# Probabilities times values of the first attention head group: one float32 product per head half instead of two split parts

## The chip, the cores and the metric

The kernel runs on one core of one Trainium2 chip. The metric is device time in microseconds (us) of one execution. Before the change three runs took 2131.02, 2131.66 and 2137.23 us, a median of 2131.66 us.

## The reference

An encoder of two layers over 1024 tokens of width 1024, all in float32. Each layer has three mixers side by side, an output projection, and a gated feed-forward part. The part that the change touches is the windowed attention: eight query heads in two groups of four, each group with one key/value head of width 64, and a window of three blocks of 128 tokens.

```python
kb, vb = bands(k), bands(v)                      # three neighbouring blocks of 128
qb = q.reshape(b, nb, BLOCK, N_KV_HEADS, grp, HEAD_DIM)
scores = jnp.einsum('bnqhgd,bnjhd->bnhgqj', qb, kb) * (HEAD_DIM ** -0.5)
probs = jax.nn.softmax(jnp.concatenate([scores, sink_b], axis=-1), axis=-1)[..., :-1]
out = jnp.einsum('bnhgqj,bnjhd->bnqhgd', probs, vb)
...
x = x + rmsnorm(concat([rmsnorm(y_f), rmsnorm(y_a), rmsnorm(y_m)]) @ w_out)
gate, up = jnp.split(rmsnorm(x) @ w_ffn_in, 2, axis=-1)
x = x + rmsnorm((silu(gate) * up) @ w_ffn_out)
```

## The kernel before

The tokens are worked in eight tiles of 128. Large products keep float32 accuracy with operands split in two: `split` (L149) writes the rounded high part with ScalarE (L151) and the rest with a subtraction on VectorE or GpSimd (L152), both in the type fp32r, and the product is the sum of the products of the parts. Working memory is two hand-placed arenas, `arena_r` (fp32r) and `arena_f` (float32), in which `at(k, ...)` and rings of places k name the buffers; a pool `big` holds more. PSUM has four pools of two banks: `sc`, `pT`, `av`, `pd`.

A layer runs in stages. After the Fourier mixer, the key/value and query products and the memory attention comes the stage of **head group 0** of the window attention, woven by `weave` with the projection of the Fourier and memory parts (tile `mo`, L162, results to the DRAM buffer `pmd`). Then follows the stage of **head group 1**, written out tile by tile together with the projection of the attention part (`mo` again, L1008), the residual and two norms (L324, L325, L284, L289), the transposes of the normed tile (`hTp`, L1033), and sums for the feed-forward part. That part begins with products named `qy`, `qz`, `qx`, `qw` (L1104), whose weights are loaded into places of arena_f that tiles 5 and 6 leave free, and summed on VectorE (L1094).

Each attention unit n of a group does the scores (`sc`, L728), masks and maxima on VectorE (L729, L735), exponentials on ScalarE (L741), and the division on GpSimd (L752). One unit later `att_values` (L756) takes for each of two or three key blocks j the transposes of four heads into one bank `pT` (L765), brings them to SBUF, and multiplies with the values into `av`. There are 22 key blocks for a group in a layer, 88 in all. The two groups do that last step differently:

- **Group 0**: `split` of the 128x512 block (high part on ScalarE, L151; low part on VectorE, L152), then two fp32r products of 128x512 (L780), whose stationary operand holds the high and the low part of the values side by side. So rows 0 to 63 of `av` hold the product with one part, rows 64 to 127 with the other. `fold` (L795) copies one half with ScalarE (L801) and adds the other with VectorE (L802), twice per unit, and thereby puts even heads into partitions 0 to 63 and odd heads into 64 to 127.
- **Group 1**: one copy by ScalarE (L770) that sorts even and odd heads, then two float32 products of 128x256 (L773) with the 64 columns of the float32 values, one for the even heads into the partitions 0 to 63 of `av` and one for the odd heads into 64 to 127. One copy by ScalarE (L782) ends the unit. The float32 values are made in advance by `values_32` (L786) on GpSimd (L791).

A float32 product stands in the profile as two matmul records, so a pair of products (even and odd heads) is four records of L773.

The order of instructions on each engine is chosen by the compiler's scheduler from the program order, the dependencies and its own estimate of durations. Every engine then works off its own queue in that order.

Of the kernel before, what the change touches and what calls it, by code (L numbers as in the profile page):

```python
# [68 lines left out]
def tile_encoder(ctx: ExitStack, tc: tile.TileContext, T, C, out):  # L69
# [51 lines left out]
    def run(k, n, step):  # L121
        return Ring(*[k + i * step for i in range(n)])
# [12 lines left out]
    mps, phs, yys = run(24, 2, 4), run(16, 3, 4), run(104, 2, 4)  # L135
# [332 lines left out]
    class Mix:  # L468
# [288 lines left out]
        def att_values(self, g, n, es_, dst):  # L757
# [4 lines left out]
            for j in range(nk):  # L762
# [3 lines left out]
                if g:  # L766

                    pf = self.pfs[self.pfi % 4]
                    self.pfi += 1
                    nc.scalar.copy(pf, pT.rearrange("p (k s) q -> p s k q", s=2))  # L770
                    for s in range(2):
                        rhs = pf[:, s].rearrange("p k q -> p (k q)")
                        mm(av[64 * s : 64 * s + 64, 0 : 2 * P], self.v32[:, k0 + j], rhs, start=j == 0, stop=j == nk - 1)  # L773
                    continue
                pp = phs(2, 512, dt=F32R)
                ph, pl = pp[:, 0], pp[:, 1]
                split(ph, pl, pT.rearrange("p h q -> p (h q)"))
                lhs = self.vst[(k0 + j) // 4][:, (k0 + j) % 4, g].rearrange("p a d -> p (a d)")
                for i, p_ in enumerate((ph, pl)):
                    mm(av, lhs, p_, start=j == 0 and i == 0, stop=j == nk - 1 and i == 1)  # L780
            if g:
                nc.scalar.copy(dst, av[:, 0 : 2 * P].rearrange("p (k q) -> p k q", k=2))  # L782
            else:
                self.fold(av, dst)

        def values_32(self):  # L786

            self.v32 = at(4, NT, HD)
            for half in range(2):
                v = self.vst[half][:, :, 1]  # L790
                nc.gpsimd.tensor_tensor(out=self.v32[:, 4 * half : 4 * half + 4], in0=f32(v[:, :, 0]), in1=f32(v[:, :, 1]), op=ALU.add)  # L791
            pf = big(4, 2, 2, P, dt=F32)
            self.pfs, self.pfi = [pf[:, i] for i in range(4)], 0

        def fold(self, av, dst):  # L795

            cut = lambda ap: ap.rearrange("p (h s q) -> p s h q", s=2, q=P)
            avh, avl = cut(av[0:64]), cut(av[64:128])
# [133 lines left out]
        def fm_load(self):  # L932
            sqs.ks = (16, 18)
            self.wfm = self.load_wout((0, 1, 6, 7))
# [520 lines left out]
```

## Time and profile before

| what | value |
|---|---|
| median of three runs | 2131.66 us |
| the profiled execution, time | 2135.5 us |
| its span, first to last instruction | 2133.7 us |
| mean granted TensorE clock | 0.969 |
| TensorE matmul busy | 2013.2 us, 94% of the span |
| VectorE busy | 1577.7 us, 74% |
| ScalarE busy | 1060.6 us, 50% |
| GpSimd busy | 863.4 us, 40% |

The profile names PE (TensorE matmul), PEld (its weight loads), DVE (VectorE), ACT (ScalarE), POOL (GpSimd), SP (SyncE) and L-numbers, which are lines of the kernel before. A timeline row is: start, length, engine, line, operation, output tile, inputs, shapes, number of instructions merged, and in brackets how long the engine was idle before and what ended that. In layer 0 the stage of group 0 lies at about 228 to 306 us of the span and that of group 1 at 306 to 410 us; in layer 1 at about 1285 to 1363 us and 1363 to 1475 us.

### The profile page before, as it was taken

To read this page: it belongs to the slowest core of one execution; us is meant where nothing else is said; L and a number is where in the kernel's file an instruction comes from. 1 tells how busy PE (TensorE), PEld (TensorE's weight loads), DVE (VectorE), ACT (ScalarE), POOL (GpSimd) and SP (SyncE) were. 2 spreads that over 40 slices of the span, in tenths; PEclk is the share of its full clock that TensorE was granted. 3 is DMA by queue.
4 is the path that set the end of the run, shared out by engine and by line. 5 is a ranking of instruction groups with operands and counts; after the bars stand their busy time and mean duration, and the time that the engine had idled before them with its cause. 6 is when DMAs were issued, how large, how long until landed. Compare 5 with 4: busy or idle time off the path is not lost.

```text
span 2133.7 us, 28334 instructions
## 1 busy us (share of the span) xinstructions
PE 2013.2 (94%) x9490; PEld 1655.0 (78%) x9490; DVE 1577.7 (74%) x2441; ACT 1060.6 (50%) x2257; POOL 863.4 (40%) x858
## 2 busy tenths in 40 slices
PE   7998999699999999999989989996999999999997
PEld 6887887478888887878868768775888888878785
DVE  7568756898877877657875686578987787876774
ACT  6467776553333334444544677776433333345441
POOL 4244446653423434213453444475442333431322
PEclk9998999899999999999989989998999999999998
DMA  6112123422332326968731122243232232378874
GB/s 221 45 50 65 65 94 105 152 65 94 118 101 95 112 94 194 318 221 287 246 138 41 60 64 85 75 137 110 84 129 94 94 111 92 123 249 284 276 261 138
DMA packets 173602, 287.50 MB, mean 135 GB/s; under 512 B 15480, under 2 KB 73360, under 8 KB 173456
## 3 DMA queue, kind: packets, MB, share of 16 engines
q1 hardware_dynamic: 165392, 266.82, 38.1%
q10 hardware_dynamic: 8064, 18.88, 2.3%
q8 instruction: 74, 1.21, 0.2%
q14 instruction: 72, 0.59, 0.1%
HBM read 219.06 MB, written 66.58 MB: 134 GB/s over the span
## 4 chain that ended last, share of the span: by engine, by line
PE 74%; DMA 8%; DVE 7%; ACT 4%; POOL 4%; issue 2%; SPq 0%; POOLq 0%; DVEq 0%; ACTq 0%
PE fo L1232 12%; PE qz L1104 11%; PE qx L1104 11%; PE qy L1104 11%; PE mo L162 7%; PE qw L1104 5%; PE kvp L162 4%; PE qp L162 3%; DVE arena_r L152 3%; DMA arena_f<-actd 2%; PE sc L728 2%; PE pT L765 2%; DMA arena_f<-in_w_ffn_out 1%; ACT arena_r L151 1%; PE zT L162 1%
## 5 line engine op out<-in xcount | busy, mean ns | idle before, releaser
L151 ACT CAST arena_r<-arena_f 128x512 fp32r<-128x512 f32 (+1 forms) x780 | 443.1, 591 | 674.0 <-PE qz L1104 115.5
L152 DVE TENSOR_TENSOR arena_r<-arena_f,arena_r 128x512 fp32r<-128x512 f32 (+1 forms) x676 | 536.6, 816 | 182.9 <-ACT arena_r L151 179.6
L1232 PE MATMUL fo<-arena_r 128*128 128x512 f32 x1848 | 432.2, 395 | 17.5 <-ACT arena_r L151 15.1
L1232 PEld LDWEIGHTS fo<-arena_r 128*128 128x128 f32 x1848 | 351.7, 191 | 94.6 <-ACT arena_r L151 17.7
L1104 PE MATMUL qy<-arena_r 128*128 128x512 f32 x1056 | 261.5, 397 | 27.6 <-ACT arena_r L151 16.5
L1104 PEld LDWEIGHTS qy<-arena_r 128*128 128x128 f32 x1056 | 201.5, 192 | 72.0 <-ACT arena_r L151 17.0
L1094 DVE TENSOR_TENSOR arena_f<-arena_f 128x512 f32<-128x512 f32 x220 | 206.0, 939 | 5.1
L1104 PE MATMUL qz<-arena_r 128*128 128x512 f32 x704 | 196.3, 389 | 1.8 <-DVE arena_r L152 1.8
L1124 POOL TENSOR_TENSOR arena_f<-arena_f 128x512 f32<-128x512 f32 x44 | 73.0, 1658 | 292.8 <-ACT arena_f L1109 292.8
L1216 POOL TENSOR_TENSOR arena_f<-arena_f 128x512 f32<-128x512 f32 x50 | 73.6, 1475 | 269.5 <-DVE arena_r L152 136.2
L1104 PEld LDWEIGHTS qz<-arena_r 128*128 128x128 f32 x704 | 132.0, 188 | 29.8 <-DVE arena_r L152 2.4
L1156 POOL TENSOR_TENSOR arena_f<-arena_f 128x512 f32<-128x512 f32 x44 | 73.6, 1674 | 165.6 <-DVE arena_f L1136 119.1
L152 POOL TENSOR_TENSOR arena_r<-arena_f,arena_r 128x256 fp32r<-128x256 f32 (+2 forms) x104 | 88.8, 859 | 118.4 <-ACT arena_r L151 93.3
L1104 PE MATMUL qx<-arena_r 128*128 128x512 f32 x528 | 127.7, 389 | 1.4 <-ACT arena_r L151 1.4
L1104 PE MATMUL qw<-arena_r 128*128 128x512 f32 x528 | 127.6, 389 | 0.0
L1104 PE MATMUL qx<-big,arena_r 128*128 128x512 f32 x528 | 126.8, 389 | 0.0
L1104 PEld LDWEIGHTS qx<-arena_r 128*128 128x128 f32 x528 | 99.1, 188 | 22.5 <-ACT arena_r L151 2.0
L1104 PE MATMUL qz<-big,arena_r 128*128 128x512 f32 x352 | 115.5, 389 | 0.0
L1104 PEld LDWEIGHTS qw<-arena_r 128*128 128x128 f32 x528 | 99.1, 188 | 20.8
L1104 PEld LDWEIGHTS qx<-big,arena_r 128*128 128x128 f32 x528 | 99.1, 188 | 20.6
L162 PE MATMUL mo<-arena_r 128*128 128x512 f32 x384 | 102.6, 406 | 5.5 <-POOL arena_r L152 4.0
L162 PE MATMUL mo<-big,arena_r 128*128 128x512 f32 x384 | 102.3, 404 | 0.0
(223 smaller groups left out, 3558.1 us busy)
## 6 DMA issues: line engine op xcount, KB each, us to landing
arena_f<-in_w_ffn_out SPq DMA_DIRECT2D x264, 256.0 KB, 4.3
arena_f<-in_w_ffn_in SPq DMA_DIRECT2D x88, 512.0 KB, 3.6
actd<-arena_f SPq DMA_DIRECT2D x154, 256.0 KB, 3.7
arena_f<-actd SPq DMA_DIRECT2D x154, 256.0 KB, 4.2
arena_f<-in_w_in SPq DMA_DIRECT2D x40, 256.0 KB, 2.7
arena_f<-in_x SPq DMA_DIRECT2D x16, 512.0 KB, 4.1
arena_f<-in_w_out SPq DMA_DIRECT2D x32, 256.0 KB, 2.8
pmd<-arena_f ACTq DMA_DIRECT2D x32, 256.0 KB, 2.0
```

Of the source, the lines that this page charges most:

```text
L151: nc.scalar.copy(hi, src)
L152: return (lo_eng or nc.vector).tensor_tensor(out=lo, in0=src, in1=f32(hi), op=ALU.subtract)
L162: mm(self.dst, a, b, start=self.i == 0, stop=self.i == self.n - 1)
L728: mm(pt, lhs, self.kst[g][i][:, k0 * P : k1 * P], start=i == 0, stop=i == 1)
L765: nc.tensor.transpose(pT[:, h, :], es_[h // 2][:, h % 2, j * P : j * P + P], ident)
L1094: nc.vector.tensor_tensor(out=s, in0=a, in1=b, op=op)
L1104: mm(pt, a, b, start=start and n == 0, stop=n == 11, skip_group_check=not start)
L1124: nc.gpsimd.tensor_tensor(out=self.v, in0=self.v, in1=self.s2, op=ALU.add)
L1156: (G if i in (0, 3) else V).tensor_tensor(out=a[i], in0=c, in1=g[i], op=ALU.mult)
L1216: (nc.vector, nc.gpsimd)[k % 2].tensor_tensor(out=s, in0=x, in1=y, op=op)
L1232: mm(pt, ab[:, 0, x, sl], ab[:, 1, y], start=new and first and j == 0, stop=last and j == 2, skip_group_check=not new)
```

## The change

Group 0 now takes the path of group 1: one copy by ScalarE of the transposed block, two float32 products per key block into the two partition halves, one copy of 128x256 at the end. The split, the two fp32r products and `fold` go. `values_32` is called for each group: for group 0 it puts the float32 values at place 18 of arena_f, in a place that the exponentials of the memory attention used before; three buffers for the copied blocks lie at 56, 58 and 6. The ring of squares in `fm_load` moves from (16, 18) to (16, 17).

```diff
-    mps, phs, yys = run(24, 2, 4), run(16, 3, 4), run(104, 2, 4)
+    mps, yys = run(24, 2, 4), run(104, 2, 4)
...
-                if g:
-
-                    pf = self.pfs[self.pfi % 4]
-                    self.pfi += 1
-                    nc.scalar.copy(pf, pT.rearrange("p (k s) q -> p s k q", s=2))
-                    for s in range(2):
-                        rhs = pf[:, s].rearrange("p k q -> p (k q)")
-                        mm(av[64 * s : 64 * s + 64, 0 : 2 * P], self.v32[:, k0 + j], rhs, start=j == 0, stop=j == nk - 1)
-                    continue
-                pp = phs(2, 512, dt=F32R)
-                ph, pl = pp[:, 0], pp[:, 1]
-                split(ph, pl, pT.rearrange("p h q -> p (h q)"))
-                lhs = self.vst[(k0 + j) // 4][:, (k0 + j) % 4, g].rearrange("p a d -> p (a d)")
-                for i, p_ in enumerate((ph, pl)):
-                    mm(av, lhs, p_, start=j == 0 and i == 0, stop=j == nk - 1 and i == 1)
-            if g:
-                nc.scalar.copy(dst, av[:, 0 : 2 * P].rearrange("p (k q) -> p k q", k=2))
+
+                pf = self.pfs[self.pfi % len(self.pfs)]
+                self.pfi += 1
+                nc.scalar.copy(pf, pT.rearrange("p (k s) q -> p s k q", s=2))
+                for s in range(2):
+                    rhs = pf[:, s].rearrange("p k q -> p (k q)")
+                    mm(av[64 * s : 64 * s + 64, 0 : 2 * P], self.v32[:, k0 + j], rhs, start=j == 0, stop=j == nk - 1)
+            nc.scalar.copy(dst, av[:, 0 : 2 * P].rearrange("p (k q) -> p k q", k=2))
+
+        def values_32(self, g):
+
+            self.v32 = at((18, 4)[g], NT, HD)
+            for half in range(2):
+                v = self.vst[half][:, :, g]
+                nc.gpsimd.tensor_tensor(out=self.v32[:, 4 * half : 4 * half + 4], in0=f32(v[:, :, 0]), in1=f32(v[:, :, 1]), op=ALU.add)
+            if g == 0:
+                self.pfs = [at(k, 2, 2, P) for k in (56, 58, 6)]
             else:
-                self.fold(av, dst)
...
+                pf = big(4, 2, 2, P, dt=F32)
+                self.pfs = [pf[:, i] for i in range(4)]
+            self.pfi = 0
...
         def fm_load(self):
-            sqs.ks = (16, 18)
+            sqs.ks = (16, 17)
...
+        mix.values_32(0)
         weave(mix.att_units(0), fm[:6] + [mix.out_load] + fm[6:])
...
-        mix.values_32()
+        mix.values_32(1)
```

The scheduler's order moves with it. Three places of it follow; line numbers in rows of the kernel after are 16 less than before from here on (L162 and L728 stay, L925 becomes L909, L1033 becomes L1017, L1104 becomes L1088, L1051 becomes L1035, L1063 becomes L1047).

TensorE, layer 0, head group 0, the values of unit 3 (`av`) among projections (`mo`), scores (`sc`) and sums of squares (`ssp`). Before:

```order
L162 MATMUL mo_2348<-big_2017,arena_r 128x512 x3
L728 MATMUL sc_2534<-arena_r 128x384 x2
L162 MATMUL mo_2356<-big_1996,arena_r 128x512 x3
L162 MATMUL mo_2356<-big_2003,arena_r 128x512 x3
L728 MATMUL sc_2634<-arena_r 128x384 x2
L780 MATMUL av_2489<-arena_r 128x512 x6
L925 MATMUL ssp_2594<-const,arena_f 128x2 x2
L162 MATMUL mo_2443<-big_2010,arena_r 128x512 x3
```

After:

```order
L772 MATMUL av_2474<-arena_f 64x256
L728 MATMUL sc_2513<-arena_r 128x384 x2
L728 MATMUL sc_2607<-arena_r 128x384 x2
L772 MATMUL av_2474<-arena_f 64x256
L909 MATMUL ssp_2573<-const,arena_f 128x2
L162 MATMUL mo_2347<-big_1996,arena_r 128x512 x3
L162 MATMUL mo_2347<-big_2003,arena_r 128x512 x3
L909 MATMUL ssp_2573<-const,arena_f 128x2
L162 MATMUL mo_2428<-big_2010,arena_r 128x512 x3
L162 MATMUL mo_2428<-big_2017,arena_r 128x512 x3
L772 MATMUL av_2474<-arena_f 64x256 x4
```

One run of six fp32r products of full width has become three runs of half-width products, of which the first two are the two halves of one pair. A run here is a stretch of half-width products with nothing of another shape between. Counted over the whole order, group 0 has 21 runs for 22 pairs in layer 0 (two pairs are torn) and 20 runs for 22 pairs in layer 1. Group 1, whose code is unchanged, goes from 19 runs to 14 in layer 0 (one pair torn before, none after) and from 19 to 20 in layer 1.

TensorE, layer 0, from the last projections of the attention part (`mo`) to the first feed-forward products (`qy`); the three pairs of `hTp` rows are the transposes of tiles 5, 6 and, beyond the last row, 7. Before:

```order
L162 MATMUL mo_3985<-arena_r 128x512 x2
L925 MATMUL ssp_3889<-const,arena_f 128x2 x2
L162 MATMUL mo_3971<-arena_r 128x512 x4
L162 MATMUL mo_3985<-arena_r 128x512 x4
L1033 MATMUL hTp_4015<-const,arena_f 128x128 x4
L1033 MATMUL hTp_4021<-const,arena_f 128x128 x4
L1104 MATMUL qy_4041<-arena_r 128x512 x2
L1033 MATMUL hTp_4068<-const,arena_f 128x128 x4
L1033 MATMUL hTp_4074<-const,arena_f 128x128 x4
L1104 MATMUL qy_4041<-arena_r 128x512 x22
L1104 MATMUL qy_4096<-arena_r 128x512 x2
```

After:

```order
L1017 MATMUL hTp_3971<-const,arena_f 128x128 x4
L1017 MATMUL hTp_3977<-const,arena_f 128x128 x4
L162 MATMUL mo_3927<-arena_r 128x512 x2
L162 MATMUL mo_3941<-arena_r 128x512 x2
L909 MATMUL ssp_3845<-const,arena_f 128x2 x2
L162 MATMUL mo_3927<-arena_r 128x512 x4
L162 MATMUL mo_3941<-arena_r 128x512 x4
L1088 MATMUL qy_3997<-arena_r 128x512 x12
L1017 MATMUL hTp_4024<-const,arena_f 128x128 x4
L1017 MATMUL hTp_4030<-const,arena_f 128x128 x4
L1088 MATMUL qy_3997<-arena_r 128x512 x12
L1088 MATMUL qy_4052<-arena_r 128x512 x2
```

The transposes of tile 5 have moved ahead of the last twelve projections, and 12 instead of 2 feed-forward products stand ahead of the transposes of tile 6, 14 instead of 24 ahead of those of tile 7. In layer 1 the counts 12 and 14 are the same, but the transposes of tile 5 stay behind all projections.

GpSimd at the same place of layer 0: the second norm of tile 5 (`nrsv`, `nrs`) and two sums for the feed-forward part (`L1051`, `L1063`). Before:

```order
L325 TENSOR_TENSOR arena_f<-arena_f 128x1024
L929 TENSOR_TENSOR grs_3771<-ms_3769,const 128x1
L1051 TENSOR_TENSOR arena_f<-big_3450,big_3942 128x512
L208 TENSOR_SCALAR nrsv_3846<-nss_3843 128x1
L210 TENSOR_TENSOR nrs_3848<-nrsv_3846,const 128x1
```

After:

```order
L325 TENSOR_TENSOR arena_f<-arena_f 128x1024
L913 TENSOR_TENSOR grs_3727<-ms_3725,const 128x1
L208 TENSOR_SCALAR nrsv_3802<-nss_3799 128x1
L210 TENSOR_TENSOR nrs_3804<-nrsv_3802,const 128x1
L1035 TENSOR_TENSOR arena_f<-big_3406,big_3898 128x512
```

The norm of tile 5 no longer stands behind a sum of 128x512.

More of the change, by code (lines that the diff above doesn't have):

```diff
@@ L786, in values_32 @@
[L786 to L798, printed above, removed]
-            for s in range(2):
-                d = dst[64 * s : 64 * s + 64]
-                nc.scalar.copy(d, avl[:, s])
-                nc.vector.tensor_tensor(out=d, in0=avh[:, s], in1=d, op=ALU.add)
+                pf = self.pfs[self.pfi % len(self.pfs)]
```

## The prediction, written before the changed kernel had run

> **What bounds the kernel now.** I read the page first, then the table of engine time by stage, then the groups of instructions within the stage that changes, then TensorE's timeline there.
>
> ```profile
> PE 2013.2 (94%) x9490; PEld 1655.0 (78%) x9490; DVE 1577.7 (74%) x2441; ACT 1060.6 (50%) x2257; POOL 863.4 (40%) x858
> ```
>
> TensorE is busy for 94% of the span, so the question for each stage is whether it is one of those where TensorE sets the pace. The stage table (columns: stretch, its length, then busy time and count of PE, PEld, DVE, ACT, POOL, then granted clock, DMA share, GB/s) answers it for group 0 in the two layers and for the end of the group 1 stage in layer 0:
>
> ```profile
> 228.00:306.00 78.00, 78.00 (x418) 66.86 (x418) 52.20 (x160) 55.49 (x148) 31.38 (x54) 0.99 0.29 102
> 366.00:410.00 44.00, 30.67 (x157) 22.45 (x155) 35.88 (x48) 27.43 (x63) 35.22 (x38) 0.89 0.42 134
> 1290.00:1360.00 70.00, 69.97 (x374) 59.37 (x373) 46.52 (x143) 49.45 (x133) 27.40 (x47) 1.00 0.28 97
> ```
>
> In the group 0 stage TensorE is never idle (78.00 of 78.00 us, 69.97 of 70.00) while VectorE works 52.20 us of 78 and ScalarE 55.49. Whatever the change takes from VectorE and ScalarE there is already hidden; whatever it adds to TensorE is paid. The end of the next stage is another matter: there TensorE is idle for 13 us of 44.
>
> **What VectorE and ScalarE lose.** The same stage of layer 0 by groups (columns: count, then busy time and mean length in ns, then idle time before):
>
> ```profile
> L780 PE MATMUL av<-arena_r 128*128 128x512 f32 x44 | 14.7, 412 | 0.0
> L152 DVE TENSOR_TENSOR arena_r<-pT,arena_r 128x512 fp32r<-128x512 f32 x22 | 14.5, 683 | 4.5 <-ACT arena_r L151 4.5
> L802 DVE TENSOR_TENSOR arena_f<-av,arena_f 64x256 f32<-64x256 f32 x16 | 6.6, 415 | 1.5 <-ACT arena_f L801 1.3
> ```
>
> 22 low parts and 16 additions go: 14.5 + 6.6 = 21.1 us of VectorE in a layer. Of ScalarE's two copies in a unit one remains, wider. No TensorE time waits on them, since it has no idle time. I cost this part at **0**; TensorE's own work is the cover, and without it the 21.1 us a layer could count.
>
> **What TensorE pays.** A matmul's listed length overlaps the next one, so prices are read from one start to the next, at full clock.
>
> ```profile
> 255.52 0.51 PE L728 MATMUL sc<-arena_r 128*128 128x384 f32 x2
> 255.88 1.55 PE L780 MATMUL av<-arena_r 128*128 128x512 f32 x6
> 257.26 0.51 PE L925 MATMUL ssp<-const,arena_f 128*128 128x2 f32 x4
> 257.63 1.62 PE L162 MATMUL mo<-big,arena_r 128*128 128x512 f32 x6
> 259.09 0.51 PE L728 MATMUL sc<-arena_r 128*128 128x384 f32 x2
> ```
>
> Six old value products take 257.26 - 255.88 = 1.38 us, 0.23 each. Two scores take 0.36. Four sums of squares and six projections take 1.83; less six times 0.23, the four take 0.45. The new product is not in group 0's trace, but group 1 runs the very same form:
>
> ```profile
> 313.08 2.01 PE L162 MATMUL mo<-arena_r 128*128 128x512 f32 x8
> 315.03 0.65 PE L773 MATMUL av<-big,arena_f 128*64 128x256 f32 x4
> 315.61 0.61 PE L925 MATMUL ssp<-const,arena_f 128*128 128x2 f32 x4
> 316.14 0.65 PE L773 MATMUL av<-big,arena_f 128*64 128x256 f32 x4
> 316.73 0.61 PE L728 MATMUL sc<-arena_r 128*128 128x384 f32 x2
> 317.27 0.65 PE L773 MATMUL av<-big,arena_f 128*64 128x256 f32 x4
> 317.85 1.20 PE L765 MATMUL pT<-const,arena_f 128*128 128x128 f32 x9
> ...
> 360.97 1.08 PE L773 MATMUL av<-big,arena_f 128*64 128x256 f32 x8
> 361.99 0.44 PE L1033 MATMUL hTp<-const,arena_f 128*128 128x128 f32 x2
> ```
>
> Four records are one pair. From 313.08 to 317.85 are 4.77 us; less eight projections (1.84), the sums of squares (0.45) and two scores (0.36), three lone pairs took 2.12 us, **0.71 each**. Two pairs in one run took 361.99 - 360.97 = 1.02, a lone one 315.61 - 315.03 = 0.58, so a pair inside a run costs 0.44 and being a run of its own costs 0.71 - 0.44 = **0.27** more. A half torn from its pair has no row here; it lies between half a pair and a whole one, and I count it whole, since nothing runs beside it.
>
> So a pair costs 0.44 where two old products cost 0.46: nothing is won by the product, and each run adds 0.27. The order of the kernel after has, for group 0:
>
> - layer 0: 21 runs, 20 whole pairs and 4 lone halves: 21 x 0.27 + 24 x 0.44 - 44 x 0.23 = 5.67 + 10.56 - 10.12 = +6.1 us
> - layer 1: 20 runs, 22 pairs: 5.40 + 9.68 - 10.12 = +5.0 us
>
> Together **+11.1 us**. With 0.14 for a run (only 0.58 - 0.44, what shows inside it) it would be +5.8; with 0.38 (the 1.95 - 1.84 = 0.11 that the projections before 315.03 took too long, paid at the way out as well) +15.6.
>
> Group 1's runs change too: 19 to 14 in layer 0 with one torn pair less (-5 x 0.27 - 0.44 = -1.8), 19 to 20 in layer 1 (+0.3): **-1.5 us**, or -0 in layer 0 if another engine is late there.
>
> The Trainium skill, "TensorEngine Tiling (Array Packing)", promises up to twofold speed for a left operand of at most 64 columns in its section "Overview", and says in "Tiling Modes" (Key Properties) that a change of the tiling mode drains the array. By the first alone the pairs would run beside each other and runs would be free; the trace agrees with the drain, since a lone pair took 0.71 us and one inside a run 0.44. The page gives no figure for the drain.
>
> **GpSimd.** `values_32(0)` adds two additions a layer ahead of the stage.
>
> ```profile
> L791 POOL TENSOR_TENSOR arena_f<-arena_r x4: 732/734/736, 209.6 to 1268.0; 128x256 f32<-128x256 f32 x4
> 215.33 1.85 POOL L852 TENSOR_SCALAR arena_f<-arena_f,rden 128x256 f32<-128x256 f32 x4 [2.09 <-DVE rden L850]
> 1274.82 1.85 POOL L852 TENSOR_SCALAR arena_f<-arena_f,rden 128x256 f32<-128x256 f32 x4 [2.67 <-DVE rden L850]
> 323.21 2.35 POOL L325 TENSOR_TENSOR arena_f<-arena_f 128x1024 f32<-128x1024 f32 x1
> ```
>
> Each takes 0.73 us. They wait for transposes of the memory attention that free place 18, and behind them stand the last divisions (L852), which TensorE transposes next. GpSimd was idle for 2.09 and 2.67 us just before those, room for one or both: **0**, at worst 0.73 us in layer 0, where the second stands between the last two divisions. Place 18 now holds values until group 0's last product, so the load of the first tile's x into places 16 to 19 is released a little later; x is first read at 323.21 (L325), some 17 us into the next stage, and SP's queue keeps its order up to the last tile's loads: 0.
>
> **Where the stage chain ends.** After the last projections the order differs most. TensorE's waits there, in layer 0 and then in layer 1:
>
> ```profile
> 399.52 1.46 PE L1033 MATMUL hTp<-const,arena_f 128*128 128x128 f32 x8
> 409.06 1.22 PE L1104 MATMUL qy<-arena_r 128*128 128x512 f32 x2 [8.07 <-ACT arena_r L151]
> ...
> 420.67 5.07 PE L1104 MATMUL qy<-arena_r 128*128 128x512 f32 x14 [4.69 <-ACT arena_f L1109]
> 425.57 0.60 PE L1033 MATMUL hTp<-const,arena_f 128*128 128x128 f32 x4
> ```
>
> ```profile
> 1458.95 1.22 PE L1104 MATMUL qy<-arena_r 128*128 128x512 f32 x2 [8.43 <-ACT arena_r L151]
> ...
> 1471.38 5.42 PE L1104 MATMUL qy<-arena_r 128*128 128x512 f32 x14 [3.83 <-ACT arena_f L1109]
> 1476.64 0.60 PE L1033 MATMUL hTp<-const,arena_f 128*128 128x128 f32 x4
> ```
>
> And VectorE's second norms of tile 5, tile 7 (layer 0) and tile 7 (layer 1), which feed these transposes:
>
> ```profile
> 393.49 2.28 DVE L289 SCALAR_TENSOR_TENSOR arena_f<-arena_f,nrs 128x1024 f32<-128x1024 f32 x1 [0.44 <-POOL nrs L210]
> ...
> 419.80 1.27 DVE L289 SCALAR_TENSOR_TENSOR arena_f<-arena_f,nrs 128x1024 f32<-128x1024 f32 x1
> ...
> 1472.60 1.28 DVE L289 SCALAR_TENSOR_TENSOR arena_f<-arena_f,nrs 128x1024 f32<-128x1024 f32 x1
> ```
>
> Tile 7's norm ends at 419.80 + 1.27 = 421.07, but its transposes start at 425.57, behind the last of 24 `qy` products: 4.5 us late. In layer 1 it is 1476.64 - 1473.88 = 2.8 us. In the new order only 14 stand there, since ten were moved ahead of tile 6's transposes, into the time when TensorE waited. So up to 7.3 us come back. Against it: those ten take 10 x 0.23 = 2.3 us, and if they start no earlier than 409.06, tile 6 waits that long, 4.6 us in both layers. In layer 0 tile 5's norm ends at 395.77 and its transposes stood behind projections until 399.52; now they go first, up to 3.7 us earlier, and they release the load of the gate weights on which `qy` waits. In layer 1 they are not moved. I take -2.5 in layer 0 (somewhat over half of 4.5) and -0.5 in layer 1 (2.8 and 2.3 nearly cancel): **-3 us**, between -7.3 and +4.6.
>
> **Sum.** 11.1 - 1.5 - 3.0 = +6.6 us. The profiled execution, 2135.5 us, would become 2142.1; it lies 3.8 us over the median of the three runs, and so on the median's footing 2131.66 + 6.6 = **2138.3 us**. All ends at once give -3 to +20 us.
>
> **Rivals.**
>
> *The end gives all back* (not slower by what can be told; about 0.3%, 6.4 us, is what a measurement of this kernel can tell from no change). Place: tile 7's transposes in both layers. It decides if they start within a microsecond of the end of their norm. Price -7.3: 11.1 - 1.5 - 7.3 = +2.3, **2134 us**. For it: TensorE waits 13 us and more there in each layer, and the order puts work into these waits. Against: what the added `qy` wait for, the split of weights, need not come earlier, above all in layer 1.
>
> *The end gives nothing*: the moved `qy` come late and hold tile 6. 11.1 - 1.5 + 0 to 4.6 = +9.6 to 14.2, **2141 to 2146 us**. For it: the 8.43 us wait of layer 1 is for ScalarE and a load whose release isn't moved.
>
> *Runs are free* in group 0, or its operand in arena_f behaves unlike group 1's: pairs at 0.44 and no 0.27, and group 1's torn pair gone (-0.4): 0 - 0.4 - 3 = -3.4, **2128 us**. Little speaks for it: group 1's rows show the form itself. That the change frees a bound VectorE would give as much; the stage table excludes it.
>
> **How the numbers follow.** The forecast, with the end giving back part (2134.5 to 2142), gets 0.48; all given back 0.22; nothing given back 0.24; runs free 0.06. The limit for slower, 2138.05, cuts the forecast near its middle, 0.27 above and 0.21 within. Slower: 0.27 + 0.24 = 0.51. Within: 0.21 + 0.17 + 0.04 = 0.42. Faster: 0.05 + 0.02 = 0.07, where an end better than its best bound is needed. The range for 8 in 10 runs from 2130, below the first rival, to 2146.
>
> **What would show it.** Group 0's stage, from its first transposes to group 1's first value product, should be longer by some 6 and 5 us with TensorE still without idle time; lone pairs from start to next start 0.58 and 8 records about 1.02; VectorE's busy time down by about 42 us in all. Tile 7's transposes against the end of its norm decide between the cases of the end. I am wrong if idle time of TensorE appears within group 0's stage, if the runs cost less there than in group 1, or if the loop through GpSimd and VectorE in group 1's stage changes its period.

## The result and the profile after

The changed kernel takes 2148.17 us (median of four runs, 2145.81 to 2148.80) against 2131.34 us before (four runs, 2128.98 to 2137.23). The ratio is 1.0075, with a 95% interval from 1.0060 to 1.0089: 16 us slower, between 13 and 19. The forecast was 2138.3 us, with a range that ended at 2146.

The busy line of the page after, in the columns of the page before:

```profile
PE 2023.1 (94%) x9578; PEld 1643.5 (77%) x9578; DVE 1559.2 (73%) x2365; ACT 1052.6 (49%) x2241; POOL 860.6 (40%) x862
```

TensorE is busy 9.9 us longer than before (2013.2), VectorE only 18.5 us less (1577.7), though the operations that went took 42 us in the trace of before.

The first question is where in the program the time is lost. Group 0's stage is cut here from TensorE's first transposes of the probabilities to group 1's first value product. Of the kernel before, group 1's first product and, further on, one product of the feed-forward part in each layer, by TensorE's timeline; then the table of engine time for group 0's stage in both layers (columns as in the stage table of the prediction):

```profile
306.73 0.65 PE L773 MATMUL av<-big,arena_f 128*64 128x256 f32 x4
...
475.89 2.88 PE L1104 MATMUL qx<-big,arena_r 128*128 128x512 f32 x12
...
1363.68 0.65 PE L773 MATMUL av<-big,arena_f 128*64 128x256 f32 x4
...
1520.41 2.88 PE L1104 MATMUL qy<-arena_r 128*128 128x512 f32 x12
```

```profile
228.34:306.73 78.39, 78.39 (x420) 66.94 (x418) 52.50 (x161) 55.22 (x149) 31.77 (x55) 0.99 0.28 101
...
1284.19:1363.68 79.49, 79.46 (x424) 67.21 (x424) 52.68 (x164) 57.67 (x158) 33.27 (x57) 1.00 0.28 96
```

The same places of the changed kernel:

```profile
309.31 0.65 PE L772 MATMUL av<-big,arena_f 128*64 128x256 f32 x4
...
480.58 2.88 PE L1088 MATMUL qx<-big,arena_r 128*128 128x512 f32 x12
...
1370.61 0.65 PE L772 MATMUL av<-big,arena_f 128*64 128x256 f32 x4
...
1530.74 2.88 PE L1088 MATMUL qy<-arena_r 128*128 128x512 f32 x12
```

```profile
226.07:309.31 83.24, 82.44 (x451) 60.69 (x450) 33.37 (x121) 52.79 (x144) 32.12 (x56) 1.00 0.28 92
...
1286.57:1370.61 84.04, 84.01 (x465) 62.62 (x465) 35.43 (x125) 53.52 (x150) 34.77 (x60) 1.00 0.24 88
```

VectorE's work in the stage falls from 52.5 to 33.4 us in layer 0 and from 52.7 to 35.4 in layer 1, and the stage grows by 4.85 and 4.55 us all the same, with TensorE at work all but 0.8 us of it. In layer 0 twelve projections of 0.231 us that stood in the stage now run after it, and in layer 1 four scores of 0.176: for the same content the stage is **7.6 us and 5.3 us longer, 12.9 in all**.

Behind it, from group 1's first product to the same product of the feed-forward part, layer 0 takes 480.58 - 309.31 = 171.27 us instead of 475.89 - 306.73 = 169.16, layer 1 160.13 instead of 156.73. That is +2.11 and +3.40, less the 2.77 and 0.70 of work that has come over: -0.7 and +2.7, **+2.0 in all**. The two parts make 14.9 us, within the interval of the runs. (The first product of the feed-forward output projection, `fo`, L1232 before and L1216 after, is as much later: 847.78 instead of 843.09 us and 1903.38 instead of 1893.05. It is used below where two kernels order the feed-forward part differently.)

### The profile page after: what moved, and what is told of

It reads as the page before. It is cut to its first block, busy times and chain, and to the rows that moved or that the text cites. A ratio compares the mean times of both kernels' runs of the same rounds, so it can differ in the third digit from the quotient of the medians.

```text
span 2145.9 us, 28387 instructions
## 1 busy us (share of the span) xinstructions
PE 2023.1 (94%) x9578; PEld 1643.5 (77%) x9578; DVE 1559.2 (73%) x2365; ACT 1052.6 (49%) x2241; POOL 860.6 (40%) x862
## 4 chain that ended last, share of the span: by engine, by line
PE 72%; DMA 8%; DVE 8%; ACT 4%; POOL 4%; issue 3%; SPq 0%; POOLq 0%; DVEq 0%; ACTq 0%
PE fo L1216 12%; PE qz L1088 11%; PE qx L1088 11%; PE qy L1088 10%; PE mo L162 6%; PE qw L1088 5%; PE kvp L162 4%; PE qp L162 3%; DVE arena_r L152 3%; DMA arena_f<-actd 3%; PE av L772 2%; PE sc L728 1%; PE pT L765 1%; PE zT L162 1%; ACT arena_r L151 1%
## 5 line engine op out<-in xcount | busy, mean ns | idle before, releaser
L1216 PE MATMUL fo<-arena_r 128*128 128x512 f32 x1848 | 433.0, 396 | 18.8 <-ACT arena_r L151 15.6
L1216 PEld LDWEIGHTS fo<-arena_r 128*128 128x128 f32 x1848 | 352.4, 191 | 96.0 <-ACT arena_r L151 18.2
L1088 PE MATMUL qy<-arena_r 128*128 128x512 f32 x1056 | 264.7, 400 | 29.5 <-ACT arena_r L151 25.1
L1088 PEld LDWEIGHTS qy<-arena_r 128*128 128x128 f32 x1056 | 203.1, 193 | 74.8 <-ACT arena_r L151 26.7
L1088 PE MATMUL qz<-arena_r 128*128 128x512 f32 x704 | 195.6, 389 | 0.0
L1088 PEld LDWEIGHTS qz<-arena_r 128*128 128x128 f32 x704 | 132.1, 188 | 27.5
L1088 PE MATMUL qw<-arena_r 128*128 128x512 f32 x528 | 128.1, 390 | 0.2 <-DVE arena_r L152 0.2
L1088 PE MATMUL qx<-arena_r 128*128 128x512 f32 x528 | 127.7, 389 | 0.0
L1088 PE MATMUL qx<-big,arena_r 128*128 128x512 f32 x528 | 127.1, 389 | 0.0
L1088 PEld LDWEIGHTS qw<-arena_r 128*128 128x128 f32 x528 | 99.0, 188 | 21.5 <-DVE arena_r L152 1.0
L1088 PE MATMUL qz<-big,arena_r 128*128 128x512 f32 x352 | 115.5, 389 | 0.0
L1088 PEld LDWEIGHTS qx<-arena_r 128*128 128x128 f32 x528 | 99.1, 188 | 20.8 <-ACT arena_r L151 0.2
L1088 PEld LDWEIGHTS qx<-big,arena_r 128*128 128x128 f32 x528 | 99.1, 188 | 20.6
L162 PE MATMUL mo<-arena_r 128*128 128x512 f32 x384 | 102.7, 404 | 3.4 <-POOL arena_r L152 2.6
L162 PE MATMUL mo<-big,arena_r 128*128 128x512 f32 x384 | 102.6, 407 | 0.0
```

Source lines behind the costliest of these rows:

```text
L162: mm(self.dst, a, b, start=self.i == 0, stop=self.i == self.n - 1)
L1088: mm(pt, a, b, start=start and n == 0, stop=n == 11, skip_group_check=not start)
L1216: mm(pt, ab[:, 0, x, sl], ab[:, 1, y], start=new and first and j == 0, stop=last and j == 2, skip_group_check=not new)
```

## The experiments

In six of the twelve (new_g0_old_order, old_g0_new_order, relief_only, one_run_a_unit, norm_first, tail_relief) the order of the instructions is held: the order in which each engine works them off, from the start of group 1 to the first feed-forward quads, is written into the kernel as a table, in both layers, and each instruction is tied behind its predecessor on its engine. This shows an effect of group 0 without what the scheduler makes of it further on. In the other six the scheduler is free, and its order moves with the edit. The kind of a dependency is written short in the cuts of code (NO_SYNC, SYNC).

```diff
+ORDERS = [{"PE": "5-6 9-10 13-14 17-18 72-73 ...", "DVE": "...", "Activation": "...", "Pool": "...", "SP": "..."}, {...}]
...
+    for m, orders in zip(marks, ORDERS):
+        base = int(traced[m].name[2:])
...
+            for a, b in zip(ks, ks[1:]):
+                tc.add_manual_dep(by[f"I-{base + b}"], f"I-{base + a}", NO_SYNC, reason="order")
```

Line numbers shift a little in such kernels (L765 becomes L783, L1088 becomes L1106 or L1110).

### Group 0's change with the old order behind it

> The changed kernel, but every engine's order from the start of group 1 to the first feed-forward quads is held, in both layers, to that of the kernel before. Theory 'products': most of the +16 us is TensorE's own work in the group 0 stages, which the two traces put at 7.7 us (layer 0) and 4.9 us (layer 1); so 2131.3 + 12.6 = about 2144 us (ratio 1.0055 to 1.006), some 3.5 us under the changed kernel. Rival 'order': the new order behind group 0 makes most of it; then the old order gives it back, 2134 to 2137 us.

Measured: 2151.49 us, ratio 1.0089 (1.0076 to 1.0102). The stage table of this kernel for group 0's stage:

```profile
227.31:314.12 86.81, 86.04 (x463) 64.46 (x462) 33.63 (x123) 51.41 (x141) 31.49 (x54) 0.98 0.26 92
...
1296.94:1380.40 83.46, 82.15 (x458) 60.91 (x456) 33.55 (x124) 50.44 (x139) 31.50 (x54) 1.00 0.27 92
```

The stages are 8.4 and 4.0 us longer than before; in layer 1 twelve projections (2.8 us) stand ahead of it, so 8.4 + 6.7 = 15 us for the same content. Some 0.7 of it is clock: the eight transposes and four scores that open the stage of layer 0 take 2.98 us here (227.31 to 230.29) and 2.26 before (228.34 to 230.60). Behind the stages nothing is lost: from group 1's first product to the same later products it takes 169.02 us (before 169.16) and 157.18 (156.73). So the time is made in group 0, and the old order behind it gives none of it back. The theory 'order' falls. 'Products' had the place right and the size too small: 15 us in the stages instead of 12.6, and 2151.49 us instead of about 2144; the part of this run's loss that lies neither in nor right behind the stages is not explained.

### The old group 0 with the new order behind it

> The kernel before, but from the start of group 1 to the first feed-forward quads held to the order of the changed kernel, in both layers. Theory 'products': the order alone costs what the traces show behind group 0, -0.35 + 0.95 in group 1 and -0.4 + 1.6 at its ends, +2 to +4 us: 2133 to 2135 us (1.001 to 1.002). Rival 'order': +11 to +13 us, 2142 to 2144 us.

Measured: 2142.61 us, 1.0043 (1.0032 to 1.0055), +9 us, between the two expectations; the sum does not tell the theories apart. The trace shows one thing behind the stages. From group 1's first product to `fo` it takes 540.17 us (303.63 to 843.80) and 532.74 (1369.90 to 1902.64) where the kernel before takes 536.36 and 529.37: 3.8 and 3.4 us more. The changed kernel has 2.1 and 3.4 more there, new_g0_old_order -0.1 and 0.5. So what the changed kernel loses behind group 0 comes with the new order, whichever group 0 stands ahead of it. In layer 0, 2.8 us of it are the twelve projections that this order moves out of group 0's stage, which is 76.19 us long here (227.44 to 303.63) instead of 78.39. How the rest of the 9 us comes about stays open.

### VectorE's relief alone

```diff
-                split(ph, pl, pT.rearrange("p h q -> p (h q)"))
+                nc.scalar.copy(ph, pT.rearrange("p h q -> p (h q)"))
+                pl = ph
...
                 nc.scalar.copy(d, avl[:, s])
-                nc.vector.tensor_tensor(out=d, in0=avh[:, s], in1=d, op=ALU.add)
```

> The kernel before without the low part (both products of a block take the high part) and without the addition of fold: the low part of the probabilities and one half of av are left out of the result. TensorE does the same products, VectorE 21.1 us less in a layer; the order behind group 0 is held to that of the kernel before. Theory 'TensorE sets the pace': 2131.3 us, within 2 us. Rival 'VectorE holds group 0': 5 to 20 us faster.

Measured: 2127.88 us, 0.9985 (0.9973 to 0.9996), 3.2 us faster. The stages themselves:

```profile
228.46:306.63 78.17, 78.17 (x420) 66.47 (x418) 33.78 (x123) 54.84 (x149) 31.67 (x55) 1.00 0.30 102
...
1280.43:1359.72 79.29, 79.26 (x424) 67.13 (x424) 35.30 (x126) 57.07 (x158) 33.26 (x57) 1.00 0.30 101
```

With 18.7 us less of VectorE the stage of layer 0 is 78.17 us instead of 78.39, that of layer 1 79.29 instead of 79.49. TensorE, not VectorE, sets the pace there; 0.4 us is all that the relief is worth. The rest of the 3.2 us lies outside the stages that were touched, and is not explained by the edit.

### One run of half-width products for a unit

```diff
+                last = nc.scalar.copy(pf, pT.rearrange("p (k s) q -> p s k q", s=2))
...
+                    prods.append(mm(av[64 * s : 64 * s + 64, 0 : 2 * P], ...))
+            for p_ in () if g else prods[:-2]:
+                tc.add_manual_dep(p_.ins, last.ins.name, SYNC, reason="one run")
```

> As new_g0_old_order, but in group 0 a unit's value products wait for the copy of its last block, so that they stand in one run: 9 runs instead of 21 in layer 0 (one torn pair instead of two), 8 instead of 20 in layer 1. Theory 'runs have a price': 24 x 0.27 + 0.44 = 6.9 us less than new_g0_old_order, about 2137 us (1.003). Rival 'the half-width product itself is dear': within 1 us of new_g0_old_order. A loss against it would mean that TensorE waits for the last copy.

Measured: 2137.01 us, 1.0024 (1.0015 to 1.0032): 14 us less than new_g0_old_order. The stages:

```profile
227.31:308.43 81.12, 80.85 (x463) 63.68 (x461) 33.11 (x123) 51.67 (x142) 31.95 (x56) 1.00 0.28 98
...
1283.50:1362.37 78.87, 78.35 (x457) 62.31 (x456) 32.39 (x124) 50.00 (x139) 31.20 (x54) 1.00 0.27 96
```

Against new_g0_old_order, with the same instructions, the stages are 5.7 and 4.6 us shorter, 10.3 us for 23 runs and one torn pair fewer. By the traces 21 + 19 runs stood there (in layer 1 one less than in the changed kernel) and 9 + 8 stand here. Two parts of it are not the runs'. 1.3 us are TensorE's waits (0.77 + 1.31 us there, 0.27 + 0.52 here). And new_g0_old_order ran the opening of layer 0's stage, eight transposes and four scores, at half clock (granted clock 0.50 there, 1.00 here):

```profile
227.31:230.29 2.98, 2.98 (x13) 2.98 (x12) 2.14 (x8) 1.79 (x5) 0.00 (x0) 0.50 0.00 0
```

```profile
227.31:228.91 1.60, 1.60 (x14) 1.52 (x12) 1.04 (x5) 1.57 (x5) 0.56 (x2) 1.00 0.00 0
```

The same instructions take 2.98 us there and 1.60 here, 1.4 us. The other 7.6 us, less 0.44 for the torn pair, make **0.31 us a run**. Against the kernel before the stages are longer by 2.7 and, with the twelve projections, 2.1 us; that is what 17 runs still cost. The product itself is not dear, its runs are: 'runs have a price' holds, with a price above the 0.27 us that it was given. The 4 us by which the run gained more than its stages lie outside them, and are not explained by the edit.

### Fewer runs in group 1

The same dependency in group 1 of the kernel before, whose other code stays (its order is free):

> The kernel before, but a unit's value products in group 1 wait for the copy of the unit's last block: 16 runs instead of 38, no torn pair. Theory 'every run costs 0.33 us in neighbours and drain, as the group 0 stages showed': 22 x 0.33 + 0.44 = 7.7 us less, 2124 us (0.9965). Rival 'another engine sets the pace of group 1': within 2 us of before; or slower, if TensorE waits for the last copy.

Measured: 2133.37 us, 1.0011 (0.9999 to 1.0023). Nothing is won with 22 runs less. What TensorE waited for in layer 0 from 300 to 432 us, before and then here (columns: total us, number of waits, longest):

```profile
PE pT L765 <- POOL arena_f L752: 0.6, 2, 0.4
```

```profile
PE pT L766 <- POOL arena_f L752: 3.7, 3, 1.5
```

The time set free turns into waits of the transposes for GpSimd's division (0.6 us before, 3.7 now). In layer 1 the first feed-forward product waits longer for its weights, 11.3 us instead of 8.4. From group 1's first product to `fo` layer 0 takes 1.8 us less than before (305.20 to 839.72 us), layer 1 6.1 more (1358.41 to 1893.89). Since the order was free and moved too, this does not show that a run costs nothing in group 1; it shows that TensorE's time saved there need not come out as time of the kernel.

### One run a unit in both groups

The same dependency in both groups of the changed kernel, order free:

> The changed kernel with one run a unit in both groups, no order held: 33 runs instead of 75. Theory 'runs': 42 x 0.33 + 3 x 0.44 = 15 us less than the changed kernel, 2132 us, level with before, since the pair itself (0.44) costs what two old products do (0.46). Rival 'the new order costs by itself': 2137 to 2142 us.

Measured: 2136.22 us, 1.0022 (1.0010 to 1.0034), between the two expectations. It stands where one_run_a_unit stands, which has 38 runs in group 1 instead of 16. That fits the last two runs, in which group 0's runs counted and nothing was won with group 1's; with the order free it does not prove it.

### Both groups on the split path

Group 1 gets `split` and `fold` as group 0 had them, with two buffers for the parts where it had four for the copied blocks; the order is free.

```diff
-                if g:
-                    pf = self.pfs[self.pfi % 4]
...
+                if g:
+                    pp = self.pps[self.pfi % 2]
+                    self.pfi += 1
...
-            if g:
-                nc.scalar.copy(dst, av[:, 0 : 2 * P].rearrange("p (k q) -> p k q", k=2))
-            else:
-                self.fold(av, dst)
+            self.fold(av, dst)
```

> The kernel before, but group 1 on the split path too (two buffers for the parts, fold at the end), so no half-width product at all. Theory 'runs and TensorE': 38 runs x 0.33, one torn pair and 44 pairs x 0.44 go, 88 products x 0.23 come: -12.5 - 0.4 - 19.4 + 20.2 = -12 us, 2119 us (0.9945). Rival 'VectorE': its 21 us a layer come back in group 1, where GpSimd and VectorE set part of the pace: 2131 to 2145 us.

Measured: 2148.37 us, 1.0081 (1.0064 to 1.0097), the rival's case and 3 us above its range. The 85 us from group 1's first product in layer 0, before and then here, by the stage table:

```profile
306.73:391.73 85.00, 82.46 (x477) 61.98 (x477) 52.98 (x108) 58.65 (x152) 58.52 (x76) 1.00 0.32 105
```

```profile
305.40:390.40 85.00, 75.51 (x411) 62.75 (x411) 67.42 (x141) 60.89 (x155) 54.70 (x75) 0.98 0.32 109
```

VectorE works 67.4 us instead of 53.0, and TensorE's busy time falls from 82.46 to 75.51 us. (The counts, 477 and 411, do not compare: a key block has four records on the float32 path and two on the split path.) In layer 0 the longest waits of the scores there end on VectorE, 2.7 us on the addition of `fold` and 1.9 on the low part of `split`. From group 1's first product to `fo` the layers take 3.9 us (305.40 to 845.66) and 9.2 us (1364.18 to 1902.71) longer than before. So the work that it is worth nothing to take away in group 0 is paid for in group 1; how much of these 13 us is VectorE's, and how much the fewer buffers' and the new order's, was not separated.

### The end of the stage: tile 7's norm, and VectorE's work

The prediction expected time back at the end of group 1's stage. There, in the kernel after, VectorE's and then TensorE's timeline (layer 0, then layer 1):

```profile
428.31 1.27 DVE L289 SCALAR_TENSOR_TENSOR arena_f<-arena_f,nrs 128x1024 f32<-128x1024 f32 x1
...
1476.90 1.29 DVE L289 SCALAR_TENSOR_TENSOR arena_f<-arena_f,nrs 128x1024 f32<-128x1024 f32 x1 [0.72 <-POOL nrs L210]
```

```profile
411.32 1.22 PE L1088 MATMUL qy<-arena_r 128*128 128x512 f32 x2 [7.52 <-ACT arena_r L151]
414.11 4.63 PE L1088 MATMUL qy<-arena_r 128*128 128x512 f32 x10 [1.56 <-DVE arena_r L152]
418.54 1.41 PE L1017 MATMUL hTp<-const,arena_f 128*128 128x128 f32 x8
...
429.73 1.09 PE L1017 MATMUL hTp<-const,arena_f 128*128 128x128 f32 x4 [1.22 <-DVE arena_f L289]
...
1485.29 1.22 PE L1088 MATMUL qy<-arena_r 128*128 128x512 f32 x2 [4.20 <-ACT arena_r L151]
1486.31 1.05 PE L1017 MATMUL hTp<-const,arena_f 128*128 128x128 f32 x4
```

In layer 0 the transposes of tile 7 now start as soon as their norm ends (428.31 + 1.27 = 429.58, start 429.73); the 4.5 us that they stood late before are gone. But the norm ends 120.3 us after group 1's first product instead of 114.3 (421.07 - 306.73), 5.9 us later. Up to there VectorE is busy 88.1 us instead of 80.2, with 147 operations instead of 139:

```profile
306.73:421.07 114.34, 95.64 (x524) 71.76 (x524) 80.17 (x139) 73.89 (x180) 80.53 (x94) 0.94 0.37 120
```

```profile
309.31:429.58 120.27, 100.79 (x549) 75.59 (x548) 88.10 (x147) 75.68 (x183) 83.04 (x96) 0.94 0.35 116
```

So the new order has put more of VectorE's work ahead of this norm. In layer 1 the norm ends 2.6 us earlier against group 1's first product, but the transposes stand behind two `qy` products that waited 4.2 us, and start 8.1 us after their norm (1478.19). VectorE's load over these ends, before and after, from the stage tables:

```profile
392.00:432.00 40.00, 21.92 (x81) 16.16 (x79) 35.88 (x42) 20.54 (x38) 24.71 (x20) 0.79 0.40 131
1440.00:1480.00 40.00, 24.95 (x109) 19.10 (x108) 35.04 (x41) 21.37 (x40) 25.92 (x22) 0.79 0.46 149
```

```profile
397.00:437.00 40.00, 23.49 (x85) 17.26 (x84) 39.21 (x44) 22.49 (x42) 25.12 (x19) 0.74 0.39 131
...
1449.00:1490.00 41.00, 24.49 (x105) 18.54 (x102) 39.84 (x44) 21.69 (x41) 24.80 (x22) 0.76 0.45 143
```

VectorE is busy 39.2 of 40 and 39.8 of 41 us. Two theories follow: its queue holds the norm of tile 7 behind other work, or its sum of work sets the end, whatever the order. The first was tried with the changed kernel's own order, held, and one operation moved:

```diff
 ORDERS[0]["DVE"]:
- ... 1184 1249 1123 1154 1299 1182 1040 1157 ...
+ ... 1184 1040 1249 1123 1154 1299 1182 1157 ...
```

> The changed kernel with its own order, except that in layer 0 VectorE does the second norm of tile 7 five places earlier, ahead of three low parts and two weight sums. Theory 'VectorE's queue holds tile 7': the norm starts at its scale, near 425.3 instead of 428.3 us, the transposes of tile 7 come 3 us earlier, and the end of layer 0's stage 2 to 3 us (2145 to 2146 us). Rival 'VectorE's sum of work sets the end': what it passes comes as much later, the end moves by less than 1 us.

Measured: 2145.62 us (two runs; 1.0068, 1.0044 to 1.0093), too close to the changed kernel to read from the time. The trace tells:

```profile
429.79 1.22 PE L1106 MATMUL qy<-arena_r 128*128 128x512 f32 x2 [5.73 <-ACT arena_r L169]
430.81 1.05 PE L1035 MATMUL hTp<-const,arena_f 128*128 128x128 f32 x4
```

The norm starts at 426.26 us, 3 us earlier against the start of group 1, but the transposes of tile 7 come no earlier: the two `qy` products ahead of them now wait 5.7 us instead of 4.6 for weights, whose low parts and sums the norm has passed on VectorE. From group 1's first product to the feed-forward product the layer takes 0.4 us longer. So this place in the queue is not what holds the end. The second theory, with the same held order:

```diff
+            if i in (5, 1):
+                nc.scalar.copy(hi, s)
+                nc.vector.tensor_tensor(out=lo[:, :, 0:1], in0=s[:, :, 0:1], in1=f32(hi[:, :, 0:1]), op=ALU.subtract)
+                return
             split(hi, lo, s, lo_eng)
```

> The changed kernel with its own order, but VectorE writes the low part of the sums 5 and 1 of tiles 4 to 7 only in the first of 128 columns of each part (the other columns of these low parts are left out of the result): 8 of its 0.68 us operations at the end of each layer's group 1 stage shrink to some 0.1 us. Theory 'VectorE's sum of work sets the end of the stage': each layer's end comes 3 to 5 us earlier, 2138 to 2142 us (1.003 to 1.005). Rival 'the weights' load and TensorE's order set it': less than 1 us a layer, 2146 to 2148 us.

Measured: 2137.65 us, 1.0028 (1.0017 to 1.0038), 10.5 us less than the changed kernel. Its timeline:

```profile
309.67 0.65 PE L790 MATMUL av<-big,arena_f 128*64 128x256 f32 x4
...
477.67 2.65 PE L1110 MATMUL qx<-big,arena_r 128*128 128x512 f32 x11
...
1364.32 0.65 PE L790 MATMUL av<-big,arena_f 128*64 128x256 f32 x4
...
1521.18 2.20 PE L1110 MATMUL qy<-arena_r 128*128 128x512 f32 x9
```

From group 1's first product to the feed-forward product layer 0 takes 168.00 us instead of 171.27, layer 1 156.86 instead of 160.13: 3.3 us less each, 6.5 in all, for eight low parts in each layer that mostly shrink from 0.68 to 0.15 us, some 4 us of VectorE. In the changed kernel VectorE's sum of work sets the end of the stage. The rest of the 10.5 us lies where both kernels do the same, and is not explained by the edit: from the second layer's first `fo` product to the end this trace takes 236.3 us, that of the changed kernel 242.5 and that of relief_only 237.8, so single executions differ there by some us.

### Three tries at a faster kernel

If VectorE's sum sets the end, work can be taken from it or moved behind the end. In the kernel before, with the order free, the low parts of sum 5 were given to GpSimd (`hb.sum(5, i - NT, nc.gpsimd)`), and the sums 1, or 5 and 1, of tiles 4 to 7 were written behind the transposes:

```diff
-                for n in (5, 1):
-                    hb.sum(n, i - NT)
+                hb.sum(5, i - NT)
...
-        for n in (7, 3):
+        for n in (1, 7, 3):
```

> The kernel before, but the low parts of sum 5 of tiles 4 to 7 are made by GpSimd. Theory 'VectorE's sum sets the end': 4 x 0.68 us less for VectorE in a layer, 2 to 5 us faster in all, 2126 to 2129 us (0.998 to 0.999). Rival 'GpSimd is as late': its operation takes about twice as long and slows VectorE beside it, 2131 to 2137 us.

> The kernel before, but sum 1 of tiles 4 to 7 (an addition and a low part each, 1.3 us of VectorE) stands in the program behind the transposes of all tiles instead of beside each tile. Theory 'VectorE's sum sets the end of group 1's stage': less of it stands ahead of tile 7's norm, 1 to 3 us a layer earlier, 2126 to 2129 us (0.998 to 0.999). Rival 'it is only shifted': the product that takes sum 1 then waits for it, 2131 us or more.

> As sum1_late, with sum 5 behind all transposes too (another low part a tile). Theory 'VectorE's sum': 0.5 to 1.5 us a layer more than sum1_late, 2124 to 2128 us. Rival 'only shifted': the first products after qy wait for sum 5, slower than sum1_late by 1 to 3 us a layer.

Measured: 2148.40 us (1.0080, 1.0064 to 1.0096), 2143.84 us (1.0055, 1.0039 to 1.0072) and 2143.35 us (1.0061, 1.0048 to 1.0074). All three are slower, the first beyond both of its expectations, and none beats the kernel before. By the traces most of the loss lies in layer 1: from group 1's first product to `fo` it takes 12.0, 6.1 and 6.1 us more than before, layer 0 0.7, 1.8 and 1.8. How much of it is the edit's own and how much the new order's was not separated, so these runs do not tell whether VectorE's sum sets the end in the kernel before as well.

## Why the prediction was wrong

It said +6.6 us with a range to 2146 us, and the kernel takes 2148.17. By its own steps:

| step | forecast, us | found, us |
|---|---|---|
| relief of VectorE and ScalarE in group 0 | 0 | -0.4 (relief_only, both stages; contained in the next row) |
| runs and pairs on TensorE in group 0 | +11.1 (6.1 + 5.0) | +12.9 (7.6 + 5.3) |
| group 1's runs | -1.5 (-1.8 + 0.3) | about -1.0 (-2.1 + 1.1) |
| the end of group 1's stage | -3 (-2.5 - 0.5) | about +3.0 (1.4 + 1.6) |
| sum | +6.6 | +14.9 by the traces, +16 (13 to 19) by the runs |

Rows three and four divide the +2.0 at the end of the last projection (`mo`) by the listed ends: 399.73 and 1449.66 us before, 403.80 and 1458.42 after, less the work that has come over and, in layer 0, the 0.85 us of tile 5's transposes that now stand ahead of it.

The step that failed is the fourth: the end of the stage was to give 3 us back, and it cost about 3. The price of a run was also too small, by less. These two terms are 7.8 of the 8.3 us between the forecast and the traces.

**The mechanism of group 0 was right.** The stage of group 0 is one in which TensorE sets the pace; a pair costs what two old products cost; every run costs more. Taking VectorE's work out alone did nothing there, and gathering the runs took away most of the loss.

**The price of a run was too small.** I took 0.27 us, from runs that stood between short instructions, and named 0.38 as the bound for a cost on the way out as well. That cost is there. From the changed kernel's timeline:

```profile
254.19 0.65 PE L772 MATMUL av<-arena_f 128*64 128x256 f32 x2
254.76 0.97 PE L728 MATMUL sc<-arena_r 128*128 128x384 f32 x4
...
269.69 1.54 PE L162 MATMUL mo<-big,arena_r 128*128 128x512 f32 x6
271.07 0.51 PE L728 MATMUL sc<-arena_r 128*128 128x384 f32 x2
...
282.78 0.65 PE L772 MATMUL av<-arena_f 128*64 128x256 f32 x4
283.37 1.66 PE L162 MATMUL mo<-big,arena_r 128*128 128x512 f32 x6
284.86 0.27 PE L765 MATMUL pT<-const,arena_f 128*128 128x128 f32 x1
...
1342.59 2.92 PE L162 MATMUL mo<-big,arena_r 128*128 128x512 f32 x12
1345.44 0.65 PE L772 MATMUL av<-arena_f 128*64 128x256 f32 x4
```

Six projections between other full-width work take 1.38 us (269.69 to 271.07). Right behind a run they take 1.49, 0.11 more; twelve ahead of a run take 2.85 instead of 2 x 1.38 = 2.76, 0.09 more; and a lone pair takes 0.59 to its end instead of 0.44, 0.15 more. Together 0.35 us between long instructions, and somewhat less beside sums of squares and transposes: the 41 runs of the changed kernel come to (12.9 - 0.8 of waits) / 41 = 0.29 us on average, those that one_run_a_unit took away to 0.31. The higher price and the 0.8 us of waits are the 1.8 us by which the term was too small. The Trainium skill says in "TensorEngine Tiling (Array Packing)", section "Tiling Modes" (Key Properties), that a change of the mode drains the array. The trace agrees, and shows a cost on both sides of a run and in its last product.

**Group 1's runs: near in size, not shown in cause.** The forecast took -1.8 us for five runs less and one torn pair less in layer 0 and noted that it might be 0 "if another engine is late there". The stretch did become some 2 us shorter, but so did a wait for GpSimd ahead of its last projections, before and after:

```profile
396.41 3.32 PE L162 MATMUL mo<-arena_r 128*128 128x512 f32 x8 [2.78 <-POOL arena_r L152]
```

```profile
401.69 2.11 PE L162 MATMUL mo<-arena_r 128*128 128x512 f32 x8 [0.51 <-POOL arena_r L152]
```

And group1_one_run took 22 runs away and won nothing in all: in layer 0 the transposes then waited for GpSimd's division. So the near agreement may be luck. TensorE's busy share of 97% from 306 to 392 us was not enough to call it the bound: of the 2.2 us that it waited there, 1.9 ended on GpSimd.

**The end of the stage was read from TensorE's queue alone.** The step said that ten `qy` products, moved ahead of tile 6's transposes, let tile 7's come up to 4.5 us earlier. They do come right behind their norm in layer 0, but I had not asked what decides when the norm comes. It is VectorE, busy 98% of the end: in layer 0 the new order has put 8 us more of its work ahead of that norm, and tail_relief shows that its sum of work sets the end, while the one change of its order that was tried (norm_first) did not move it. old_g0_new_order loses as much behind the stages (3.8 and 3.4 us), so the loss belongs to the order and not to the new products. In layer 1 the rival that I gave 0.24 took place: products moved ahead hold the tiles behind them. They were also dearer than the 2.3 us that I counted, since they run behind waits of 7.5 and 1.6 us:

```profile
414.00:418.50 4.50, 4.39 (x10) 3.36 (x11) 3.78 (x6) 1.69 (x4) 2.60 (x2) 0.50 0.53 161
```

The granted clock there is 0.50, and the ten take 418.54 - 414.11 = 4.43 us; over the next 4 us it is 0.90. The Trainium skill, "TensorE: Matmul & The Clock Gate", section "What's actually happening", has TensorE fall to half rate after an idle window of about 3.4 us and come back after a busy one; these rows agree.

**One execution was read.** The stages were read in one profiled execution of each kernel. That of before ran at half clock just ahead of group 0 (granted clock 0.53 from 225 to 230 us, against 1.00 in the trace of after) and reached group 0 2.3 us later than the changed kernel's did. The two traces differ by 12.2 us where the medians differ by 16.8, which is the size of what one execution against another can hide; the 2 us between the traces' sum and the runs' stay open.

Of the signs named in advance, these held: group 0's stages are longer by about the forecast with hardly any idle time; a lone pair takes 0.58 to the next start and eight records 1.02. One did not: VectorE's busy time was to fall by about 42 us and fell by 18.5. The operations are gone (2365 instead of 2441), and group 0's stages have 36.4 us less, but elsewhere VectorE is busy 17.9 us longer. The cases of the end were to be told by tile 7's transposes against their norm, and in layer 0 this sign pointed to the wrong case, because the norm itself had moved.

## What to carry to other kernels

Price a change of TensorE's shape by how often the shape changes in the order, with the neighbours on both sides, and not by its products alone: 17 runs instead of 40 took some 9 us off the two stages here, waits included, while the products stayed the same. Before work taken off an engine is counted as time won, take it away in a trial, stage by stage: the relief of VectorE was worth nothing in group 0, and giving it the same work again in group 1 came with a loss of 13 us there. Where a wait ends on one engine's queue, look for what made its input late before counting the wait as room.

## What the runs showed of the hardware that was not expected

- A lone half of a pair takes as long as a whole one: the two records at 254.19 us take 0.57 us to the next start, the four at 282.78 us 0.59. So the two half-width products of a pair run beside each other, and a torn pair costs a whole pair more.
- TensorE's transposes hide behind what follows: a single 128x128 transpose ahead of a projection takes 0.03 us to the next start (274.39 to 274.42 us in the changed kernel's timeline), against 0.11 us ahead of another transpose.
- The same opening of a stage, eight transposes and four scores, took 2.98 us in one trace (granted clock 0.50) and 1.60 in another (1.00). At this size a comparison of two traces needs the granted clock of the stretch beside the time.
